# A two-layer diffusion block in split FP32: two more units of two FFNs as seven half-size products, the sums for them earlier, the dot products of the adaptive weights later

## The chip, the cores and the metric

One core of a Trainium2 chip runs the whole program as one launch. The metric is the device time of one execution in microseconds (us). Of the kernel before three runs are shown: 1622.91, 1625.24 and 1625.51, median 1625.24.

The engines that matter here: TensorE (PE) multiplies matrices, VectorE (DVE) and ScalarE (ACT) work on elements, SyncE (SP) issues the transfers. Each executes its own instructions in the order in which they were written into its queue, and waits on semaphores for the others.

## The reference

Two layers work on 256 image tokens ("LAT" in the kernel) and 256 context tokens ("CTX"), width 1024. Each layer has an FFN, a mixer (attention, then an mLSTM) and another FFN, each followed by a normalised residual. Shifts, scales and gates come from nine "adaptive" vectors a layer, `silu(c) @ ada_w`, for two conditions.

```python
def half_ffn(h, shift, scale, gate, w_in, w_out, g, b):
    xm = modulate(h, shift, scale)
    a, u = jnp.split(xm @ w_in, 2, axis=-1)
    y = (jax.nn.silu(a) * u) @ w_out
    return post_norm(h, 0.5 * gate * y, g, b)
...
        mod_lat = jnp.split((jax.nn.silu(c) @ ada_w[i] + ada_b[i])[:, None, :], N_MOD, axis=-1)
        mod_ctx = jnp.split((jax.nn.silu(c_ctx) @ ada_w[i] + ada_b[i])[None, None, :], N_MOD, axis=-1)
```

`w_in` is 1024 x 5632 and `w_out` 2816 x 1024. All inputs are FP32.

## The kernel before

**Precision.** A product in FP32 is made of three matmuls (`mm3`, line 241): every operand is split into a high part, a cast on ACT (line 225), and a low part, a subtraction on DVE (line 230, both in `split`). High by high, high by low, low by high are added up in PSUM. The weights are split on the fly: a raw tile of 128x1024 comes in by DMA (three raw slots, tag `raw`), the parts go into one of seven buffers (tag `w`).

**An FFN.** The 2816 hidden columns are 22 units of 128 (`j`). A plain unit (`unit_in`) multiplies its columns of both halves of `w_in` with all 512 tokens: 48 matmuls with 512 columns of tokens, then `ffn_g` applies silu (ACT, line 588), the product (DVE, line 589) and splits the result. After units 0 to 10 come eight out rows (`unit_out(0, d, ...)`, 33 matmuls of 512), then units 11 to 21, and eight more out rows that end in four narrow ones for each half of the tokens, into which the next normalisation is woven. In the second and third FFN (`li` 1 and 2) the units 0 to 3 are woven into the work ahead, and units 4 to 10 run plainly.

**Half-size units.** In the second and third FFN units 11 to 21 are made by `fast_in`: the weight of a unit is a 2x2 block of (half of the input width, half of the output), the tokens are a 2x2 block of (half of the width, LAT or CTX), and seven products of half size replace eight. That is 84 matmuls of 256 columns. It takes three sums of token blocks (`made`, from `fast_sums`, lines 611 to 623) that are made once, and four sums of the weight's blocks for every unit (s1, s2, s4, s3, line 641), whose parts are then split. PE accumulates in x, y, v and z; ACT copies halves out (lines 666 to 671) and DVE adds (lines 675 to 680). `fast_sums` also replaces the CTX tokens of the lower half of the width by LAT minus CTX, so no plain unit can follow. The sums are made beside out rows 4 and 5 of the first half, in memory that the pieces of `ada_w` held till then. One of the three sums is copied by ACT into a `w` buffer for unit 11 (line 635).

**Dots.** A piece of `ada_w` (128 rows of its transpose, 512 KB) is multiplied with silu(c) and added up on DVE (`ada_dot`, line 350), once for each condition. The table `DOTS` says how many pieces are loaded beside each unit and out row; `flush` issues the dots of the pieces of the step before.

**Order.** A list scheduler writes each engine's order from the program's order, with its own idea of durations; on the chip these orders are fixed.

Of the kernel before, what the change touches and what calls it, by code (L numbers as in the profile page):

```python
# [18 lines left out]
P = 128  # L19
# [7 lines left out]
NF = 22  # L27
# [61 lines left out]
SUMSAT = 4  # L89
# [4 lines left out]
    1: {**{("in", j): 2 for j in range(11)}, **{("out", 0, d): 2 if d < 2 else 1 for d in range(4)}, **{("out", 1, d): 1 for d in range(4)}},  # L94
    2: {**{("in", j): 2 for j in range(4)}, **{("in", j): 3 if j < 9 else 2 for j in range(4, 11)}, **{("out", 0, d): 2 if d < 3 else 0 for d in range(4)},
        **{("out", 1, d): 2 if d < 3 else 1 for d in range(4)}},
# [76 lines left out]
class Body:  # L173
    def __init__(self, ctx, tc, a, out):
        self.tc, self.nc, self.a, self.out = tc, tc.nc, a, out
        self.n = 0
        self.sp = ctx.enter_context(tc.tile_pool(name="sp", bufs=1))
        self.pp = ctx.enter_context(tc.tile_pool(name="pp", bufs=1, space=PSUM))
        self.later, self.running = [], []
        self.fence = {}  # L180
        self.fine = False

        self.nraw, self.spare = 0, None

# [104 lines left out]
    def silu_c(self):  # L289

        pool = ExitStack()
        self.n += 1
        p = pool.enter_context(self.tc.tile_pool(name=f"cp{self.n}", bufs=1, side="right"))
        self.cp = p
        self.cb = self.t([P, 2, D], pool=p)
        return pool
# [5 lines left out]
    def silu_all(self):  # L302
        pool = self.silu_c()
        self.silu_load()
        self.silu()
        return pool
# [285 lines left out]
    def fast_operands(self, st):  # L592

        n = ND // 2 * TL
        x = self.t([P, 6 * n], F32R, pool=st)
        self.t([P, FLIP], pool=st)
        self.made = [[x[:, (2 * i + p) * n : (2 * i + p + 1) * n].rearrange("p (k f) -> p k f", f=TL) for p in range(2)] for i in range(3)]

    def fast_sums(self, i):
# [5 lines left out]
        def at(ks, g):  # L605
            return self.xh[:, ks, g[0] : g[1]], self.xl[:, ks, g[0] : g[1]]

        def whole(ks, g):
            o = self.tmp().rearrange("p (k f) -> p k f", k=2)
            h, l = at(ks, g)  # L610
            V.tensor_tensor(out=o, in0=h.bitcast(F32), in1=l.bitcast(F32), op=ALU.add)
# [3 lines left out]
        V.tensor_tensor(out=a, in0=a, in1=b, op=ALU.subtract)  # L615
        self.split(a, *at(lo, CTX))
# [3 lines left out]
        V.scalar_tensor_tensor(a, a, -1.0, c, ALU.mult, ALU.subtract)  # L620
        self.split(a, *made(0))
        d = whole(up, LAT)
        V.scalar_tensor_tensor(d, a, -1.0, d, ALU.mult, ALU.subtract)
        self.split(d, *made(2))

    def fast_in(self, j, w_in, st):
# [4 lines left out]
        if j == NFH:  # L631
# [17 lines left out]
        self.split(sums[:, : 2 * half], *ws[2])  # L649
        self.split(sums[:, 2 * half :], *ws[3])  # L650
# [33 lines left out]
    def ffn(self, layer, s, gate, groups, side, start=None, cpool=None):  # L684
# [4 lines left out]
        with self.tc.tile_pool(name=f"ffn{li}", bufs=1) as gp:  # L689
# [34 lines left out]
            for hf in range(2):  # L724
# [26 lines left out]
                fast = cpool is not None and hf == 1  # L751
                for j in js:
                    if fast:
                        self.fast_in(j, w_in, st)
                        continue
                    unit_in(j, stream(j), allg)
                    assert not self.running
                    if j >= LEAD + FAFTER:
                        self.fine = False
                    call("in", j)  # L760
                    self.residual(2, self.pin)
                if not hf:
# [3 lines left out]
                if fast:  # L766
                    more.close()
                    cpool = self.silu_all()
                for d in range(body):
                    if cpool and not hf and d == SUMSAT:  # L770
                        self.flush()
                        cpool.close()
                        self.n += 1
                        more = ExitStack()
                        st = more.enter_context(self.tc.tile_pool(name=f"st{self.n}", bufs=1, side="right"))
                        self.fast_operands(st)
                    unit_out(hf, d, w, allg)
                    if cpool and not hf and d >= SUMSAT and d - SUMSAT < 2:
                        self.fast_sums(d - SUMSAT)
                    call("out", hf, d)  # L780
                if body < ND:
                    w = Keep(self, w.chunks, SH, w)
                    self.fine = True
                    for g in groups:
                        for d in range(body, ND):
                            unit_out(hf, d, w, g, TAILSTEP)
                    self.steps('B')
        return cpool
# [846 lines left out]
def emit(ctx, tc, a, out):  # L1635
# [4 lines left out]
    cpool = b.silu_c()  # L1640
    both2 = (0, 1)
    queue = [(0, p, both2) for p in range(16, 72)]
    later = [(1, p, both2) for p in range(40)] + [(1, p, (0,)) for p in range(40, 72)]
    made = {}
# [8 lines left out]
    def side(key, coef, keep=(True, True), nxt=True, alone=False, dots={}):  # L1653
        def pop():
            for _ in range(3 if len(queue) > 40 else 2):
                if queue:
                    b.ada(*queue.pop(0))

        def some(n):
            b.flush()  # L1660
            for _ in range(min(n, len(later))):
                layer, dt, vecs = later.pop(0)
# [6 lines left out]
        for j in range(NF):  # L1669
            s["in", j] = (lambda j=j: some(dots.get(("in", j), 0))) if dots else pop  # L1670
        for d in range(ND):
            s["out", 0, d] = (lambda d=d: some(dots.get(("out", 0, d), 0))) if dots else pop
            s["out", 1, d] = lambda d=d: some(dots.get(("out", 1, d), 0))
# [109 lines left out]
```

## Time and profile before

| what | number |
|---|---|
| median of three runs | 1625.24 us |
| the profiled execution, its span | 1624.66 us, 1622.9 us |
| PE, DVE, ACT busy | 1608.2, 1349.3, 749.0 us |
| second FFN, units 4 to 10 | 602.08 to 678.24 us |
| second FFN, units 11 to 21 | 738.11 to 843.11 us |
| third FFN, units 11 to 21 | 1090.08 to 1195.08 us |

Times in the trace count from the span's start. A busy PE is a PE with a matmul in flight; where it waits for an operand, its row or its stretch shows less than the whole. An operation on DVE or ACT is listed with its full length, and the next can start before that has passed, so the step from start to start is read from the timeline. Names of tiles are shown without numbers in the trace (`t<-t,t`), so operations are told by line and shape.

### The profile page before, as it was taken

To read this page: it belongs to the slowest core of one execution; us is meant where nothing else is said; L and a number is where in the kernel's file an instruction comes from. 1 tells how busy PE (TensorE), PEld (TensorE's weight loads), DVE (VectorE), ACT (ScalarE), POOL (GpSimd) and SP (SyncE) were. 2 spreads that over 40 slices of the span, in tenths; PEclk is the share of its full clock that TensorE was granted. 3 is DMA by queue.
4 is the path that set the end of the run, shared out by engine and by line. 5 is a ranking of instruction groups with operands and counts; after the bars stand their busy time and mean duration, and the time that the engine had idled before them with its cause. 6 is when DMAs were issued, how large, how long until landed. Compare 5 with 4: busy or idle time off the path is not lost. (4 is left out here: it accounts for less than half of the span.)

```text
span 1622.9 us, 26548 instructions
## 1 busy us (share of the span) xinstructions
PE 1608.2 (99%) x10280; PEld 1450.3 (89%) x10280; DVE 1349.3 (83%) x2687; ACT 749.0 (46%) x1276; POOL 62.4 (4%) x77
## 2 busy tenths in 40 slices
PE   9999999999999999999999999999999999999998
PEld 7888888889988998889999998889999989999986
DVE  7899978648879879999976979689967968897597
ACT  6522132314676443316652443336642657566542
POOL 0000000001011200000000100000001000020000
PEclk9999999999999999999999999999999999999999
DMA  9677765422203347633354258723372343437562
GB/s 358 220 250 238 237 207 184 141 66 85 66 2 99 136 144 228 212 104 118 117 175 151 79 180 289 245 64 106 109 238 83 98 130 92 151 98 259 170 181 91
DMA packets 72222, 251.56 MB, mean 155 GB/s; under 512 B 7960, under 2 KB 10776, under 8 KB 72096
## 3 DMA queue, kind: packets, MB, share of 16 engines
q1 hardware_dynamic: 71520, 249.09, 48.0%
q8 instruction: 80, 1.31, 0.3%
q10 hardware_dynamic: 576, 0.79, 0.1%
q14 instruction: 46, 0.38, 0.1%
HBM read 248.79 MB, written 1.05 MB: 154 GB/s over the span
## 5 line engine op out<-in xcount | busy, mean ns | idle before, releaser
L241 PE MATMUL t<-t,t 128*128 128x256 f32 (+2 forms) x8340 | 1307.7, 318 | 3.2 <-ACT t L225 1.1
L241 PEld LDWEIGHTS t<-t,t 128*128 128x128 f32 x8340 | 1175.8, 188 | 120.7 <-ACT t L225 2.0
L225 ACT CAST t<-t 128x1024 fp32r<-128x1024 f32 (+3 forms) x509 | 421.6, 850 | 479.3 <-PE t L241 225.0
L230 DVE TENSOR_TENSOR t<-t,t 128x256 fp32r<-128x256 f32 (+2 forms) x728 | 505.4, 729 | 110.7 <-ACT t L225 106.9
L350 DVE SCALAR_TENSOR_TENSOR t<-t,t 128x1024 bf16<-128x1024 f32 x224 | 260.7, 1220 | 0.0
L588 ACT ACTIVATE t<-t 128x512 f32<-128x512 f32 (+1 forms) x71 | 34.4, 489 | 98.8 <-PE t L241 97.8
L941 PE MATMUL t<-t,t 128*128 128x256 f32 (+1 forms) x256 | 79.3, 310 | 0.2 <-ACT t L541 0.2
L718 DVE SCALAR_TENSOR_TENSOR t<-t,t,t 128x256 f32<-128x256 f32 x96 | 42.7, 478 | 43.9 <-PE t L241 43.7
L943 PE MATMUL t<-t,t 128*128 128x256 f32 (+1 forms) x256 | 78.5, 307 | 0.1
L942 PE MATMUL t<-t,t 128*128 128x256 f32 (+1 forms) x256 | 78.3, 306 | 0.1
L589 DVE TENSOR_TENSOR t<-t,t 128x512 f32<-128x512 f32 (+1 forms) x71 | 39.0, 553 | 40.6 <-PE t L241 27.7
L484 POOL TENSOR_TENSOR t<-t,t 128x256 f32<-128x256 f32 x30 | 23.2, 774 | 1105.1 <-ACT t L474 1103.8
L869 PE MATMUL t<-t,t 128*128 128x512 f32 (+1 forms) x300 | 61.0, 364 | 0.4 <-DVE t L863 0.4
L869 PEld LDWEIGHTS t<-t,t 128*128 128x128 f32 x300 | 51.3, 189 | 10.0 <-DVE t L863 1.1
L474 ACT ACTIVATE t<-t 128x256 f32<-128x256 f32 x72 | 26.1, 412 | 65.8 <-DVE t L467 65.8
L1470 PE MATMUL t<-t,t 128*128 128x512 f32 (+2 forms) x276 | 55.7, 357 | 0.0
L1470 PEld LDWEIGHTS t<-t,t 128*128 128x128 f32 (+1 forms) x276 | 44.9, 183 | 11.0 <-issue 1.1
L942 PEld LDWEIGHTS t<-t,t 128*128 128x128 f32 x256 | 48.1, 188 | 3.3 <-DVE t L230 0.8
L941 PEld LDWEIGHTS t<-t,t 128*128 128x128 f32 x256 | 48.2, 188 | 3.2 <-ACT t L541 0.4
L943 PEld LDWEIGHTS t<-t,t 128*128 128x128 f32 x256 | 48.1, 188 | 2.8 <-DVE t L542 0.3
L541 ACT ACTIVATE t<-t,t 128x256 fp32r<-128x256 f32 x72 | 32.8, 502 | 31.1 <-DVE t L540 31.1
L641 DVE TENSOR_TENSOR t<-t,t 128x512 f32<-128x512 f32 x66 | 45.3, 687 | 0.4
(211 smaller groups left out, 1107.8 us busy)
## 6 DMA issues: line engine op xcount, KB each, us to landing
t<-in_ffn_in SPq DMA_DIRECT2D x168, 512.0 KB, 4.1
t<-in_ada_w SPq DMA_DIRECT2D x138, 512.0 KB, 4.4
t<-in_ffn_out SPq DMA_DIRECT2D x66, 512.0 KB, 4.4
t<-in_ffn_last SPq DMA_DIRECT2D x22, 512.0 KB, 3.5
t<-in_att_in SPq DMA_DIRECT2D x12, 512.0 KB, 3.5
t<-in_att_out SPq DMA_DIRECT2D x8, 512.0 KB, 3.6
t<-in_ml_qk SPq DMA_DIRECT2D x8, 512.0 KB, 3.7
t<-in_ml_v SPq DMA_DIRECT2D x8, 512.0 KB, 3.6
```

The source lines that it names most:

```text
L225: self.behind(self.nc.scalar.copy(h, x))
L230: self.behind(self.nc.vector.tensor_tensor(out=ls, in0=xs, in1=hs.bitcast(F32), op=ALU.subtract))
L241: mm = lambda *k, **kw: self.nc.tensor.matmul(*k, skip_group_check=not group, **kw)
L350: ins = nc.vector.scalar_tensor_tensor(self.tmp().bitcast(BF16), r, 1.0, self.cb[:, v, :], ALU.mult, ALU.mult, accum_out=to)
L589: V.tensor_tensor(out=sl, in0=sl, in1=pu[:, :n], op=ALU.mult)
L641: add = lambda o, x, y: V.tensor_tensor(out=o, in0=x, in1=y, op=ALU.add)
L718: V.scalar_tensor_tensor(z, y[:, gg[0] - t0 : gg[1] - t0], gate()[:, v, d : d + 1], z, ALU.mult, ALU.add)
L869: pin(nc.tensor.matmul(o, gs[g], ws[k][w][:, i : i + n], start=k == k0 and g == w == 0, stop=k == k1 - 1 and g == 1,))
L941: mm(o, self.xh[:, k, c], wh, start=k == 0, stop=False)
L942: mm(o, self.xh[:, k, c], wl, start=False, stop=False)
L943: mm(o, self.xl[:, k, c], wh, start=False, stop=k == ND - 1)
L1470: mm = lambda *k, **kw: pin(nc.tensor.matmul(*k, **kw))
```

## The change

In the second and third FFN units 9 and 10 are made by `fast_in` as well. For that the token sums (`fast_sums`) move from out rows 4 and 5 to beside units 6 and 7, and the splits of the difference LAT minus CTX, which overwrite tokens, come as `fast_first` beside unit 8, ahead of unit 9. The table `FAST` gives the first half-size unit and the unit beside which the sums start. The pieces of `ada_w` lose their memory from unit 6 on, so `DOTS` puts dots beside units 0 to 4 and then beside the out rows, where the pieces take halves of `w` buffers. Silu(c) keeps its memory and is no longer loaded again. The sums of a unit's weights are four tiles of 512 and no longer one of 2048, and two splits of 1024 become four of 512. The copy of a token sum for PE is made for units 9 and 11. In the first FFN a piece's dots now come one step behind its load.

```diff
-SUMSAT = 4
+FAST = {0: (99, 99), 1: (9, 6), 2: (9, 6)}
...
     def ada_load(self, layer, dt):
...
-        r = self.t([P, 1024], tag="ada", bufs=PIECES, pool=self.cp)
+        if self.cp:
+            r = self.t([P, 1024], tag="ada", bufs=PIECES, pool=self.cp)
+        else:
+            self.halves = self.halves or self.pair(F32)
+            r = self.halves.pop()
...
         a, b = whole(lo, LAT), whole(lo, CTX)
-        V.tensor_tensor(out=a, in0=a, in1=b, op=ALU.subtract)
-        self.split(a, *at(lo, CTX))
+        for k in range(2):
+            o = self.first[2 * i + k] = self.t([P, TL], tag="s1", bufs=S1B)
+            V.tensor_tensor(out=o, in0=a[:, k, :], in1=b[:, k, :], op=ALU.subtract)
...
+    def fast_first(self):
+        for k in range(ND // 2):
+            self.split(self.first[k], *self.x(k, CTX))
...
-        sums = self.t([P, 4 * half], tag="sums", bufs=1, pool=st)
...
-        s1, s2, s4, s3 = (part(sums, i) for i in range(4))
+        s1, s2, s4, s3 = (self.tmp() for _ in range(4))
...
-        self.split(sums[:, : 2 * half], *ws[2])
-        self.split(sums[:, 2 * half :], *ws[3])
+        for i, x in enumerate((s1, s2, s4, s3)):
+            self.split(x, *(part(y, i % 2) for y in ws[2 + i // 2]))
...
-                    if fast:
-                        self.fast_in(j, w_in, st)
-                        continue
-                    unit_in(j, stream(j), allg)
+                    if j >= fast:
+                        self.fast_in(j, w_in, j in (fast, NFH))
+                    else:
+                        unit_in(j, stream(j), allg)
...
-                    call("in", j)
+                    if j <= sums:
+                        call("in", j)
                     self.residual(2, self.pin)
+                    if j == sums:
+                        self.fast_operands()
+                    if sums <= j < sums + 2:
+                        self.fast_sums(j - sums)
+                    if j == fast - 1:
+                        self.fast_first()
...
                             unit_out(hf, d, w, g, TAILSTEP)
+                            self.flush()
```

DVE's order at the end of the second FFN's unit 8, before. Row 819 is unit 8's product (`t_6458`), rows 817, 818 and 820 are low parts of weights, rows 822 to 825 dots:

```order
817 L230 TENSOR_TENSOR t_6653<-t_6651,t_6653 128x1024
818 L230 TENSOR_TENSOR t_6682<-t_6680,t_6682 128x1024
819 L589 TENSOR_TENSOR t_6458<-t_6458,t_6397 128x512
820 L230 TENSOR_TENSOR t_6729<-t_6727,t_6729 128x1024
821 L230 TENSOR_TENSOR t_6457<-t_6458,t_6456 128x512
822 L350 SCALAR_TENSOR_TENSOR t_6463,t_6126<-t_6388,t_5394 128x1024
823 L350 SCALAR_TENSOR_TENSOR t_6465,t_6126<-t_6388,t_5394 128x1024
824 L350 SCALAR_TENSOR_TENSOR t_6467,t_6126<-t_6390,t_5394 128x1024
825 L350 SCALAR_TENSOR_TENSOR t_6469,t_6126<-t_6390,t_5394 128x1024
```

and after (lines are nine to sixteen higher). Row 831 is the last operation of the moved sums, row 833 unit 8's product; `t_6507` and `t_6509` are unit 9's raw tiles, `t_6515` the low part of a11, `t_6516` of a12 and a22, `t_6517` of s1 and s2, and lines 657 are the sums s1, s2, s4, s3:

```order
831 L231 TENSOR_TENSOR t_68<-t_6409,t_67 128x256
832 L657 TENSOR_TENSOR t_6511<-t_6507,t_6509 128x512
833 L598 TENSOR_TENSOR t_6487<-t_6487,t_6426 128x512
834 L231 TENSOR_TENSOR t_6515<-t_6507,t_6515 128x512
835 L231 TENSOR_TENSOR t_6516<-t_6509,t_6516 128x1024
836 L231 TENSOR_TENSOR t_6486<-t_6487,t_6485 128x512
837 L572 SCALAR_TENSOR_TENSOR t_66<-t_66,t_5324,t_5665 128x256 x2
838 L657 TENSOR_TENSOR t_6512<-t_6511,t_6507 128x512
839 L231 TENSOR_TENSOR t_6517<-t_6511,t_6517 128x512
840 L657 TENSOR_TENSOR t_6513<-t_6512,t_6509 128x512
841 L657 TENSOR_TENSOR t_6514<-t_6507 128x512
842 L231 TENSOR_TENSOR t_6517<-t_6512,t_6517 128x512
```

The dots are gone from here, the moved sums stand ahead of unit 8's product, and unit 9's low parts stand behind it.

Further on in DVE's order after: `t_6640` and `t_6642` are unit 10's raw tiles, `t_6649` the low part of its a12 and a22, `t_6650` of its s1; lines 691 to 696 are the end of unit 9:

```order
845 L231 TENSOR_TENSOR t_6648<-t_6640,t_6648 128x512
846 L657 TENSOR_TENSOR t_6644<-t_6640,t_6642 128x512
847 L691 TENSOR_TENSOR t_6538<-t_6538,t_6536 128x512
848 L231 TENSOR_TENSOR t_6649<-t_6642,t_6649 128x1024
849 L695 SCALAR_TENSOR_TENSOR t_6539<-t_6535,t_6539 128x512
850 L657 TENSOR_TENSOR t_6645<-t_6644,t_6640 128x512
851 L696 TENSOR_TENSOR t_6538<-t_6538,t_6539 128x512
852 L657 TENSOR_TENSOR t_6646<-t_6645,t_6642 128x512
853 L657 TENSOR_TENSOR t_6647<-t_6640 128x512
854 L231 TENSOR_TENSOR t_6633<-t_6538,t_6632 128x512
855 L572 SCALAR_TENSOR_TENSOR t_66<-t_66,t_5324,t_5665 128x256 x2
856 L231 TENSOR_TENSOR t_6650<-t_6644,t_6650 128x512
```

Unit 10's s1 has its sum in row 846 and its low part in row 856, ten rows behind. Before, a plain unit's two low parts stood here (rows like 818).

PE's order at the start of unit 9, before (`t_6480` and `t_6481` are its two sums in PSUM, `t_6484` its first weight; the third matmul takes the low part):

```order
3409 L241 MATMUL t_6480<-t_67,t_6484 128x512
3410 L241 MATMUL t_6480<-t_68,t_6484 128x512
3411 L241 MATMUL t_6480<-t_67,t_6484 128x512
3412 L241 MATMUL t_6481<-t_67,t_6484 128x512
3413 L241 MATMUL t_6481<-t_68,t_6484 128x512
```

after, from the last matmul of unit 8 on (`t_6535` is x, `t_6536` y and v, `t_6537` z, `t_6504` the copied token sum):

```order
3408 L242 MATMUL t_6426<-t_67,t_6458 128x512
3409 L242 MATMUL t_6535<-t_67,t_6515 128x256
3410 L242 MATMUL t_6535<-t_68,t_6515 128x256
3411 L242 MATMUL t_6536<-t_67,t_6516 128x256
3412 L242 MATMUL t_6536<-t_68,t_6516 128x256
3413 L242 MATMUL t_6537<-t_6504,t_6516 128x256 x2
3414 L242 MATMUL t_6535<-t_67,t_6515 128x256 x2
```

and in the middle of unit 10 (`t_6669` takes s1, `t_6670` z, `t_6668` s2, `t_6777` is the first out row):

```order
3469 L242 MATMUL t_6669<-t_67,t_6650 128x256
3470 L242 MATMUL t_6669<-t_68,t_6650 128x256
3471 L242 MATMUL t_6670<-t_6308,t_6649 128x256 x2
3472 L242 MATMUL t_6668<-t_6308,t_6650 128x256 x2
3473 L242 MATMUL t_6670<-t_6308,t_6649 128x256 x10
3474 L242 MATMUL t_6777<-t_5509,t_6780 128x512
3475 L242 MATMUL t_6777<-t_5510,t_6780 128x512
3476 L242 MATMUL t_6669<-t_67,t_6650 128x256 x2
```

Six matmuls of unit 9 that take high parts of the weights stand ahead of the first that takes a low part; in unit 10 two of s1's stand ahead of z's, s2's first two and two matmuls of the first out row, and s1's third, with the low part, behind them.

## Rows read from the trace of the kernel before

**Rows 1.** The profile's page: busy time of each engine, clock by slices.

```profile
PE 1608.2 (99%) x10280; PEld 1450.3 (89%) x10280; DVE 1349.3 (83%) x2687; ACT 749.0 (46%) x1276; POOL 62.4 (4%) x77
...
PEclk9999999999999999999999999999999999999999
```

**Rows 2.** Table of stretches: start:end length, busy (count) by engine, PEclk, DMA share, GB/s.

```profile
602.08:656.48 54.40, 54.40 (x242) 45.05 (x241) 52.45 (x85) 19.37 (x29) 0.00 (x0) 1.00 0.76 227
656.48:678.24 21.76, 21.76 (x97) 18.02 (x96) 18.61 (x33) 8.27 (x13) 0.00 (x0) 1.00 0.68 219
...
738.11:843.11 105.00, 105.00 (x926) 105.00 (x924) 97.20 (x129) 67.15 (x109) 0.00 (x0) 1.00 0.39 122
1090.08:1195.08 105.00, 105.00 (x925) 105.00 (x924) 95.44 (x128) 67.16 (x110) 0.00 (x0) 1.00 0.41 122
```

**Rows 3.** DVE's groups by form, whole span: count, then busy us, mean ns, idle before.

```profile
L230 DVE TENSOR_TENSOR t<-t,t 128x1024 fp32r<-128x1024 f32 x236 | 286.8, 1222 | 65.7 <-ACT t L225 62.7 <-PE t L241 1.7
L350 DVE SCALAR_TENSOR_TENSOR t<-t,t 128x1024 bf16<-128x1024 f32 x224 | 260.7, 1220 | 0.0
L230 DVE TENSOR_TENSOR t<-t,t 128x256 fp32r<-128x256 f32 x346 | 132.8, 426 | 40.4 <-ACT t L225 40.2
L230 DVE TENSOR_TENSOR t<-t,t 128x512 fp32r<-128x512 f32 x133 | 90.8, 686 | 4.1 <-ACT t L225 3.5
...
L563 DVE SCALAR_TENSOR_TENSOR t<-t,t,t 128x256 f32<-128x256 f32 x64 | 28.0, 479 | 0.0
```

**Rows 4.** DVE's timeline in a half-size unit: start, length, instruction [idle before <-releaser].

```profile
1102.57 0.69 DVE L641 TENSOR_TENSOR t<-t,t 128x512 f32<-128x512 f32 x1
1103.17 0.69 DVE L641 TENSOR_TENSOR t<-t 128x512 f32<-128x512 f32 x1
1103.77 0.69 DVE L230 TENSOR_TENSOR t<-t,t 128x512 fp32r<-128x512 f32 x1
```

**Rows 5.** DVE's timeline around the second FFN's units 6 to 9.

```profile
633.67 0.87 DVE L563 SCALAR_TENSOR_TENSOR t<-t,t,t 128x256 f32<-128x256 f32 x2
...
635.61 0.69 DVE L589 TENSOR_TENSOR t<-t,t 128x512 f32<-128x512 f32 x1
636.22 1.82 DVE L230 TENSOR_TENSOR t<-t,t 128x1024 fp32r<-128x1024 f32 x2
...
654.09 2.35 DVE L230 TENSOR_TENSOR t<-t,t 128x1024 fp32r<-128x1024 f32 x2
656.78 0.69 DVE L589 TENSOR_TENSOR t<-t,t 128x512 f32<-128x512 f32 x1 [0.34 <-PE t L241]
```

**Rows 6.** DVE's timeline beside the second FFN's fifth out row.

```profile
713.76 1.89 DVE L611 TENSOR_TENSOR t<-t,t 128x512 f32<-128x512 f32 x3
715.57 0.69 DVE L615 TENSOR_TENSOR t<-t,t 128x512 f32<-128x512 f32 x1
...
716.96 0.68 DVE L230 TENSOR_TENSOR t<-t,t 128x512 fp32r<-128x512 f32 x1
```

**Rows 7.** ACT's timeline at the same place.

```profile
716.29 0.62 ACT L225 CAST t<-t 128x512 fp32r<-128x512 f32 x1 [14.96 <-DVE t L615]
```

**Rows 8.** The page's DMA issues: line, KB each, us to landing.

```profile
t<-in_ffn_in SPq DMA_DIRECT2D x168, 512.0 KB, 4.1
...
t<-in_ffn_out SPq DMA_DIRECT2D x66, 512.0 KB, 4.4
```

**Rows 9.** ACT's groups by form, whole span.

```profile
L225 ACT CAST t<-t 128x1024 fp32r<-128x1024 f32 x309 | 323.4, 1051 | 388.0 <-PE t L241 220.3 <-issue 92.5 <-DMA t<-in_ffn_in 43.1
```

**Rows 10.** DVE's timeline in the second FFN's last out rows.

```profile
869.52 1.43 DVE L230 TENSOR_TENSOR t<-t,t 128x256 fp32r<-128x256 f32 x4
...
874.05 0.75 DVE L424 TENSOR_TENSOR t<-t,t 128x256 f32<-128x256 f32 x2
...
885.45 0.42 DVE L424 TENSOR_TENSOR t<-t,t 128x256 f32<-128x256 f32 x1
```

More of the change, by code (lines that the diff above doesn't have):

```diff
@@ L765, in ffn @@
                 body = ND - TAIL if hf else ND
-                if fast:
-                    more.close()
-                    cpool = self.silu_all()
+                self.halves = []
+                if hf and fast < NF:
+                    self.shut()
+                    self.cp = self.open()
                 for d in range(body):
[L770 to L776, printed above, removed]
                     unit_out(hf, d, w, allg)
-                    if cpool and not hf and d >= SUMSAT and d - SUMSAT < 2:
-                        self.fast_sums(d - SUMSAT)
                     call("out", hf, d)
+                self.halves = []
                 if body < ND:
@@ L1639, in emit @@
     b.setup_rest()
-    cpool = b.silu_c()
+    b.silu_c()
     both2 = (0, 1)
@@ L1643, in emit @@
     later = [(1, p, both2) for p in range(40)] + [(1, p, (0,)) for p in range(40, 72)]
+    later, queue = queue[56 - 0 :] + later, queue[: 56 - 0]
     made = {}
@@ L1653, in side @@
     def side(key, coef, keep=(True, True), nxt=True, alone=False, dots={}):
[L1654 to L1657, printed above, removed]
         def some(n):
             b.flush()
-            for _ in range(min(n, len(later))):
-                layer, dt, vecs = later.pop(0)
+            todo = queue or later
+            for _ in range(min(n, len(todo))):
+                layer, dt, vecs = todo.pop(0)
                 b.waiting.append((b.ada_load(layer, dt), layer, dt, vecs))
@@ L1669, in side @@
         for j in range(NF):
-            s["in", j] = (lambda j=j: some(dots.get(("in", j), 0))) if dots else pop
+            s["in", j] = lambda j=j: some(dots.get(("in", j), 0))
         for d in range(ND):
-            s["out", 0, d] = (lambda d=d: some(dots.get(("out", 0, d), 0))) if dots else pop
-            s["out", 1, d] = lambda d=d: some(dots.get(("out", 1, d), 0))
+            for hf in range(2):
+                s["out", hf, d] = lambda hf=hf, d=d: some(dots.get(("out", hf, d), 0))
         return s
     both = (LAT, CTX)
-    b.ffn(0, 0, once("g0", lambda: b.half_gate(0, 2)), both, side("n0", lambda: b.ln_mod(0, 0, (0, 3))), start)
-    assert not queue
-    cpool.close()
+    b.ffn(0, 0, once("g0", lambda: b.half_gate(0, 2)), both, side("n0", lambda: b.ln_mod(0, 0, (0, 3)), dots=DOTS[0]), start)
+    assert not queue, len(queue)
+    b.flush()
+    b.shut()
+    b.shut()
     b.attention(lambda: b.shift_(0, 5), side("n1", lambda: b.ln_mod(0, 1, (0, 6))))
-    cpool = b.silu_all()
-    cpool = b.ffn(0, 1, once("g1", lambda: b.half_gate(0, 8)), both, side("n2", lambda: b.ln_mod(0, 2, (1, 0)), dots=DOTS[1]), cpool=cpool)
-    cpool = b.ffn(1, 0, once("g2", lambda: b.half_gate(1, 2)), both, side("n3", lambda: b.ln_mod(1, 0, (1, 3)), (True, False), dots=DOTS[2]), cpool=cpool)
+    b.silu_all()
+    b.ffn(0, 1, once("g1", lambda: b.half_gate(0, 8)), both, side("n2", lambda: b.ln_mod(0, 2, (1, 0)), dots=DOTS[1]))
+    b.ffn(1, 0, once("g2", lambda: b.half_gate(1, 2)), both, side("n3", lambda: b.ln_mod(1, 0, (1, 3)), (True, False), dots=DOTS[2]))
     assert not later, len(later)
     b.flush()
-    cpool.close()
+    b.shut()
+    b.shut()
     b.mlstm(lambda: b.shift_(1, 5, slice(0, 1)), side("n4", lambda: b.ln_mod(1, 1, (1, 6), 1), alone=True))
```

56 lines of the change are left out of this document (31 added, 25 removed).

## The prediction

> **What bounds the kernel now.** First the page: TensorE (PE) is busy 99% of the span and its clock stands at full speed in nearly every slice, so a second is saved where PE gets less to do and lost where it has to wait [rows 1]. Then the table of stretches. It shows the second FFN's plain units 4 to 8 and 9 and 10, the eleven half-size units of the second FFN, and those of the third. PE is busy through all of them at a granted clock of 1.00. VectorE (DVE) is busy 52.45 of 54.40 us beside the plain units and 97.20 and 95.44 of 105.00 us beside the half-size ones [rows 2]. So PE is the bound, with DVE close behind, and DVE feeds PE: each weight's low part is a DVE subtraction that PE waits for.
>
> From the same table, 96 matmuls of 512 columns take 21.76 us, 0.2267 us each, and a plain unit (48 of them) 10.88 us. A half-size unit has 84 matmuls of 256 columns; eleven have 924 and fill 104.7 of the 105.00 us (the rest is the edge's 512-wide ones): 0.1133 us each, 9.52 us a unit [rows 2].
>
> **The gain.** Units 9 and 10 of two FFNs go from 10.88 to 9.52 us: 4 x 1.36 = 5.44 us, if PE waits no more than it did.
> [...]
>
> **DVE in a half-size unit.** Before: nine 512-wide operations and three 1024-wide ones. After: thirteen and one (two wide subtractions became four half ones). One 512-wide lasts 0.686 us, a 1024-wide 1.222, a dot 1.220 [rows 3], but in a run of 512-wide ones each starts 0.60 us after the one before [rows 4], and two 1024-wide ones take 2.35 us, so the second starts some 1.14 us behind the first [rows 5]. So 9 x 0.60 + 3 x 1.14 = 8.8 before and 13 x 0.60 + 1.14 = 8.9 after, both under 9.52: the steady run stays PE's, cost 0.
> [...]
>
> **Unit 9: late weights.** This is the main cost. Before, DVE is through with unit 6's product at 636.22 and then does weights and dots [rows 5]. DVE's order after is the same up to there; then come the sums of the tokens with what else stands between: 21 operations of 512, 6 plain and 8 three-operand ones of 256. Steps: 0.60 (the token sums beside the rows show it too: three in 1.89 [rows 6]); 0.40 for a three-operand one (a pair in 0.87, of which the last 0.479 [rows 3, 5]); 0.34 for a plain one of 256 (four in 1.43, the last 0.426 [rows 3, 10]). That is 12.6 + 2.0 + 3.2 = 17.8 us, to 654.1. The low parts inside need a cast by ScalarE (ACT) first: from the sum's start at 715.57 over the cast at 716.29 to the low part at 716.96 is 1.39 us [rows 6, 7], and two to three other operations stand between each time, so no more than 0.3 is lost.
>
> Behind these stand, in order, s1's sum for unit 9 and the product of unit 8, which can't start before unit 8 ends: 656.78, as in the row that waits for PE [rows 5]. Only behind it come unit 9's own low parts. a11: 657.38 to 658.07. PE is done with unit 8 at 656.5 and can do six half matmuls that need no low part (0.7), so it waits from 657.2 to 658.1: 0.9. Then a12 and a22 together (to 659.1), unit 8's low part (659.7), two residual operations (660.5), s2's sum, s1's low part (661.8), s4's and s3's sums, s2's low part (to 663.6). PE, late by 0.9, wants s2's at 663.2: 0.5 more. Together 1.4, say 1.5 (0.8 where a step comes earlier, 2.4 where a cast on ACT is in the way of another).
>
> **Unit 10: the same and a transfer.** Its second raw tile goes into the slot that unit 9's s4 sum reads last, done at 662.4. The transfer takes 4.1 us [rows 8], so it is there at 666.5, and s1's sum waits for it. Behind that in DVE's queue come the sum of unit 9's halves, the 1024-wide low part, the rest of unit 9's end (residual, product, its low part) and the sums s2, s4, s3: ten steps, 6.8 us, so s1's low part runs 673.25 to 673.9. PE, begun at 667.5, has 40 half matmuls and two of the first out row in front (4.5 + 0.45): 672.5. It waits 1.6. What can add: ACT casts the first out row's chunks (1.05 each, [rows 9]) between the copies out of PSUM that PE's last two products need, and these chunks are transfers of 4.4 us [rows 8]; they just fit by my walk. I take 2.0 (0.8 to 3.8). So the second FFN loses 3.5. The third has the same order with five 128x16 operations more in the chain: 4.0. Together 7.5 (3 to 12).
>
> **Token sums no longer beside out rows; dots there instead.** An out row (33 matmuls, 7.48 us) now has four dots of 1.15, two gated additions of 0.40 and 11/8 low parts of 1.14: 7.0 us, hidden, with 0.5 to spare. In the last rows a piece's dots are flushed after each 256-wide row: before, two dots stand ahead of that row's addition and the last sum for the mean is made at 885.45 [rows 10]. After, from 874.7, when the pair at 874.05 is through: four dots (4.6), an addition and a sum (0.74), four dots (4.6), two additions and sums (1.5) make 886.2 against 885.9, and PE's order has the mean's matmul later by ten half matmuls. +0.5 (0 to 1). The first FFN's dots change only when their tile is loaded: 0. Two reloads of silu(c) vanish off the path: 0.
>
> **Sum.** -5.44 + 7.5 + 0.5 = +2.6 us. The profiled execution took 1624.66, so 1627.3; the median of the runs shown, 1625.24, is 0.58 above that execution: 1627.8.
>
> **Rivals.**
> A. The weights are in time, or nearly: DVE's backlog shrinks where a wait that I counted overlaps. For it: PE has not one idle microsecond in units 4 to 10 with DVE 96% busy [rows 2], and the scheduler chose an order in which only a11's low part is late. Against it: unit 8's product can't be earlier and stands ahead. It gives -5.44 + (0 to 1.8) + 0.5: 1620.3 to 1622.1.
> B. Slower in earnest: the chain of raw slots. There are three; unit 10's second weight, then the first out row's chunks each wait for a slot that a late sum reads last. If a copy out of PSUM waits in ACT's queue behind a cast whose chunk isn't there, PE stands for the transfer's rest and the cast (up to 4.4 + 1.05 less the 2 us of work at hand, some 3.5) in each FFN: +2.6 + 7 = +9.6, 1634.8. It decides from the point where the chunk lands over 2 us later than 672. For it: seven weight buffers hold nine pairs' worth around unit 9. Against it: the chunks are asked for at 662.
> C. DVE's steps are full durations where forms alternate. 26 units of 0.6 us: +16, about 1641. The runs of [rows 4] speak against it.
>
> **Numbers.** Forecast 0.57 (stalls 3.5 to 9.5 in sum: 1623.8 to 1629.8), A 0.23, B 0.16, C 0.04. Under 0.2%, 3.25 us, a measurement can't tell from no change: 1622.0 to 1628.5 is the same. Faster: most of A, 0.18. Slower: B, C and the third of the forecast above 1628.5, 0.39. Same 0.43. The range 1621.0 to 1634.0 leaves out the best of A and the upper half of B, with C: under 2 in 10.
>
> **What would show it.** In the profile after: PE idle at the start of units 9 and 10 of both FFNs, released by DVE's low part (line 231), 1 to 2.5 us each, and no idle in the eleven units behind; DVE's unit 8 product directly before unit 9's first low part; 84 matmuls of 0.1133 us in units 9 and 10. Wrong would be: no PE idle there (A), ACT's cast or the in_ffn_out transfer as releaser of PE's waits (B), or half-size units of over 9.6 us throughout (C). Then the time falls out of the forecast's own range.

## The result, and the profile after

The changed kernel takes 1628.08 us (median of eight runs, 1625.34 to 1630.55), the kernel before 1625.03 beside it (eight runs, 1622.91 to 1626.32): a ratio of 1.0020, interval 1.0011 to 1.0030. That is 3 us slower and just inside of what was called the same; 1627.8 was forecast. Its runs spread over 5.2 us, those of before over 3.4.

Where the time went is read by cutting both traces at the same matmuls (starts of units and rows). The changed kernel was profiled twice (the second time among the experiments), the kernel before three times. Lengths in us:

| stretch | before, three profiles | changed | changed again |
|---|---|---|---|
| 2nd FFN, units 9, 10 and first out row | 29.24 each | 29.96 | 30.05 |
| units 11 to 21 | 105.00 each | 106.15 | 105.00 |
| last rows and the norm in them | 33.84 to 34.13 | 34.43 | 34.15 |
| 3rd FFN, lead (units 0 to 3) | 46.87, 46.88, 47.15 | 47.16 | 49.10 |
| units 9, 10 and first out row | 29.24 each | 29.26 | 29.36 |
| units 11 to 21 | 105.00 each | 105.38 | 105.00 |
| last rows | 33.82 to 34.12 | 34.31 | 34.49 |

All other stretches of the two FFNs agree within 0.01. Ahead of the second FFN's unit 4 and behind the third FFN one kernel's own profiles differ by up to 2.5, so nothing is read there.

The page after: PE has 144 more matmuls and 2.3 us less of busy time [rows 1], and the transfers are as long as before [rows 8].

```profile
PE 1605.9 (99%) x10424; PEld 1455.0 (90%) x10424; DVE 1376.1 (85%) x2783; ACT 768.0 (47%) x1356; POOL 62.2 (4%) x77
...
t<-in_ffn_in SPq DMA_DIRECT2D x168, 512.0 KB, 4.1
```

The same table of stretches after, for the second FFN's units 4 to 8, its units 9, 10 and first row, its run of half-size units, the third FFN's lead and its units 9, 10 and first row. PE is idle where it never was in [rows 2]: 1.54 and 1.23 us beside units 9 and 10, at a granted clock of 1.00.

```profile
601.65:656.08 54.43, 54.43 (x243) 45.05 (x241) 52.12 (x94) 21.10 (x36) 0.00 (x0) 1.00 0.36 111
656.08:686.04 29.96, 28.42 (x203) 26.29 (x201) 25.91 (x39) 20.06 (x36) 0.00 (x0) 1.00 0.53 197
738.40:844.54 106.14, 105.85 (x925) 105.65 (x924) 100.63 (x152) 69.45 (x131) 0.00 (x0) 1.00 0.36 125
908.92:956.08 47.16, 46.44 (x399) 45.94 (x397) 37.27 (x106) 22.61 (x49) 2.31 (x3) 1.00 0.36 109
1010.50:1039.76 29.26, 28.03 (x202) 25.89 (x201) 24.83 (x38) 18.05 (x34) 0.00 (x0) 1.00 0.57 224
```

PE's timeline at units 9 and 10 of the second FFN (in brackets the idle time before the row and what ended it):

```profile
657.18 13.62 PE L242 MATMUL t<-t,t 128*128 128x256 f32 x110 [0.71 <-ACT t L226]
671.25 1.65 PE L242 MATMUL t<-t,t 128*128 128x256 f32 x12 [0.45 <-ACT t L682]
673.24 27.02 PE L242 MATMUL t<-t,t 128*128 128x512 f32 x139 [0.34 <-ACT t L226]
```

In terms of single matmuls against their steps: 0.98 us before the first that takes a12, 0.32 before s2's first, 0.73 before s2's first in unit 10, 0.62 before the first out row's. These four waits, each with what the next matmul loses, make 2.65 of the 3.44 us that the stretch takes beyond 26.52 (29.24 less the gain of 2.72). Most of the rest is no wait: nearly all half-wide matmuls there start 0.118 us apart and not 0.113, at a granted clock of 1.00. DVE's timeline there answers to [rows 5]: s1's sum, unit 8's product (waiting for PE), unit 9's low parts behind it, the sums, then unit 10's s1, which waits for its transfer, the sum of unit 9, s2's sum at 668.99, and from 672.79 on s1's low part:

```profile
654.53 0.68 DVE L657 TENSOR_TENSOR t<-t,t 128x512 f32<-128x512 f32 x1
656.35 0.69 DVE L598 TENSOR_TENSOR t<-t,t 128x512 f32<-128x512 f32 x1 [1.13 <-PE t L242]
656.95 2.42 DVE L231 TENSOR_TENSOR t<-t,t 128x512 fp32r<-128x512 f32 x3
...
661.29 0.69 DVE L657 TENSOR_TENSOR t<-t,t 128x512 f32<-128x512 f32 x1
...
666.04 0.69 DVE L657 TENSOR_TENSOR t<-t,t 128x512 f32<-128x512 f32 x1 [1.02 <-DMA t<-in_ffn_in]
666.65 0.69 DVE L691 TENSOR_TENSOR t<-t,t 128x512 f32<-128x512 f32 x1
...
668.99 0.68 DVE L657 TENSOR_TENSOR t<-t,t 128x512 f32<-128x512 f32 x1
...
672.79 5.90 DVE L231 TENSOR_TENSOR t<-t,t 128x512 fp32r<-128x512 f32 x7
```

And ACT's: the two copies of the token sum, a11's cast, unit 8's silu, then a12 and a22's cast as the first of three; further on two casts, the first of which waits for s2's sum, and the copy of unit 10's x:

```profile
653.09 2.00 ACT L652 CAST t<-t 128x1024 fp32r<-128x1024 f32 x2
655.00 0.61 ACT L226 CAST t<-t 128x512 fp32r<-128x512 f32 x1
655.60 0.60 ACT L597 ACTIVATE t<-t 128x512 f32<-128x512 f32 x1
656.09 2.12 ACT L226 CAST t<-t 128x1024 fp32r<-128x1024 f32 x3
...
669.70 1.22 ACT L226 CAST t<-t 128x512 fp32r<-128x512 f32 x2 [1.56 <-DVE t L657]
670.83 0.36 ACT L682 COPY t<-t 128x256 f32<-128x256 f32 x1
```

The walk's times are hit within 0.5 us (656.35, 666.04 and 672.79 against 656.78, 666.5 and 673.25, with PE 0.43 ahead at unit 4 already). But ACT ends three of PE's four waits, not DVE: a12's high part is cast behind the copies of the last token sum, and x's copy stands behind two casts. DVE is not out of it: unit 10's x is complete at 668.9, and the first of the casts ahead of its copy waits 1.56 us for s2's sum, which stands in DVE's queue behind the late s1.

### The profile page after: what moved, and what is told of

It is laid out like the page before. It is cut to its first block, busy times and chain, and to the rows that moved or that the text cites. A ratio compares the mean times of both kernels' runs of the same rounds, so it can differ in the third digit from the quotient of the medians.

```text
span 1625.2 us, 26955 instructions
## 1 busy us (share of the span) xinstructions
PE 1605.9 (99%) x10424; PEld 1455.0 (90%) x10424; DVE 1376.1 (85%) x2783; ACT 768.0 (47%) x1356; POOL 62.2 (4%) x77
## 5 line engine op out<-in xcount | busy, mean ns | idle before, releaser
L226 ACT CAST t<-t 128x1024 fp32r<-128x1024 f32 (+3 forms) x573 | 436.9, 785 | 454.9 <-PE t L242 133.5
L231 DVE TENSOR_TENSOR t<-t,t 128x256 fp32r<-128x256 f32 (+3 forms) x792 | 517.0, 689 | 100.1 <-ACT t L226 97.1
L597 ACT ACTIVATE t<-t 128x256 f32<-128x256 f32 (+1 forms) x67 | 32.0, 483 | 98.1 <-PE t L242 97.0
L598 DVE TENSOR_TENSOR t<-t,t 128x256 f32<-128x256 f32 (+1 forms) x67 | 36.3, 545 | 36.9 <-PE t L242 31.1
L657 DVE TENSOR_TENSOR t<-t,t 128x512 f32<-128x512 f32 x78 | 53.6, 687 | 2.2 <-DMA t<-in_ffn_in 1.5
```

Of the source, the lines that this page charges most:

```text
L226: self.behind(self.nc.scalar.copy(h, x))
L231: self.behind(self.nc.vector.tensor_tensor(out=ls, in0=xs, in1=hs.bitcast(F32), op=ALU.subtract))
L598: V.tensor_tensor(out=sl, in0=sl, in1=pu[:, :n], op=ALU.mult)
L657: add = lambda o, x, y: V.tensor_tensor(out=o, in0=x, in1=y, op=ALU.add)
```

## The experiments

All runs are beside runs of the kernel before on the same chip; ratios are to those.

**e1: all but the two units.**
```diff
-FAST = {0: (99, 99), 1: (9, 6), 2: (9, 6)}
+FAST = {0: (99, 99), 1: (11, 6), 2: (11, 6)}
```


> All of the change but its units: half-size products from unit 11 on, token sums still beside units 6 and 7, dots still beside the out rows. In the changed kernel's trace the stretch from unit 9 to the end of the first out row costs, against the kernel before, +0.7 us in the second FFN and 0.0 in the third (gain 2.72 each, waits 3.4 and 2.7); what lies elsewhere costs +1.6 (1.1 and 0.4 in the two runs of units 11 to 21, 0.3 at the second FFN's tail, 0.3 in the third's lead, -0.4 ahead of unit 4). Theory 'late weights at 9 and 10, and a thin prefetch in the steady run': the units give nothing on balance, so without them the time stays 1 to 2 us above the kernel before (about 1626.5), with some 1 us of PE's waits left in the runs of units 11 to 21. Theory of the prediction alone (all of the loss at units 9 and 10, 0.5 at the tail): 0.5 us above it, 1625.5, and runs of 105.0 us. Theory 'the moved dots cost it': 3 us above it, 1628.

Measured: 1629.08 against 1625.77, ratio 1.0021 (1.0012 to 1.0031). The stretches of units 9 and 10 are 29.24 again, runs 105.00, tails 34.67 and 34.68, lead 47.29. So the units are worth nothing that shows, near what the tally in the expectation had, but the rest costs 3.4 us (1.9 to 5.0) and not 0.5: the nearest of the three was the moved dots. The profile shows 1.5 of it in the two tails and the lead; where the remainder lies, in the parts that are not read, stays open.

**e2: s3 first among a unit's weight sums.**
```diff
         add(s1, a21, a22)
         add(s2, s1, a11)
         add(s4, s2, a12)
-        add(s3, a11, a21)
```
(the removed line now stands ahead of s1's)


> The four weight sums of a half-size unit in another order: s3, s1, s2, s4 in place of s1, s2, s4, s3. Now a unit's first raw tile is read last by s2 and not by s3, it comes free before the second, and the tiles go round in the three slots: each load waits for the tile three loads back (before this edit a unit's second tile waits for the unit before's second one, two loads back). Theory 'thin prefetch': in the second FFN's run of units 11 to 21 the last load is issued several us earlier than at 822.5, ACT waits for weights there under 1 us in all (5.7 us in the changed kernel), the run takes 105.0 us and not 106.1, the third FFN's 105.0 and not 105.4; unit 10's second tile is asked for 0.6 to 1.2 us earlier, so its wait shrinks by as much in each FFN. Time 1.5 to 4 us below the changed kernel: 1624 to 1626.5. Rival 'DVE's and ACT's own order sets the late units': runs of 106 as before, time within 0.7 us of 1628.

Measured: 1639.47, ratio 1.0082 (1.0066 to 1.0098); runs of 111.05 and 108.97. The theory's forecast failed. ACT in the run, unit 20's load on its way: the cast waits for the transfer, silu and x's copy of the unit before stand behind it:

```profile
819.38 1.05 ACT L226 CAST t<-t 128x1024 fp32r<-128x1024 f32 x1 [1.04 <-DMA t<-in_ffn_in]
820.34 0.62 ACT L692 ACTIVATE t<-t 128x512 f32<-128x512 f32 x1
820.87 0.35 ACT L682 COPY t<-t 128x256 f32<-128x256 f32 x1
822.42 0.62 ACT L226 CAST t<-t 128x512 fp32r<-128x512 f32 x1 [1.20 <-DVE t L696]
```

DVE at the same time: the product behind that silu (821.71), its low part, which waits for ACT, and only then s3 and the other sums:

```profile
814.38 1.41 DVE L657 TENSOR_TENSOR t<-t,t 128x512 f32<-128x512 f32 x2
...
821.71 0.68 DVE L696 TENSOR_TENSOR t<-t,t 128x512 f32<-128x512 f32 x1
823.07 0.69 DVE L231 TENSOR_TENSOR t<-t,t 128x512 fp32r<-128x512 f32 x1 [0.69 <-ACT t L226]
823.68 0.68 DVE L657 TENSOR_TENSOR t<-t 128x512 f32<-128x512 f32 x1
824.28 1.41 DVE L657 TENSOR_TENSOR t<-t,t 128x512 f32<-128x512 f32 x2
```

The last sum (s2) frees the raw slot, and the load for it is issued at 825.76; the one before was issued at 815.85. So load, cast, silu, product, low part, sums and the next load make a ring of 9.91 us, longer than a unit's 9.52, and PE waits for x's copy:

```profile
832.40 4.37 PE L242 MATMUL t<-t,t 128*128 128x256 f32 x36 [0.73 <-ACT t L682]
...
843.92 6.42 PE L242 MATMUL t<-t,t 128*128 128x256 f32 x51 [1.22 <-ACT t L682]
```

The order of four additions thus sets the pace of 11 units: with this edit a unit's first load follows the one before after 9.90 or 9.91 us at most places of both runs. In the changed kernel the ring is just short enough: where transfers take 3.4 to 3.6 us, that step is 9.32 or 9.33 us at most places, 0.2 less than a unit. So a long transfer can show (106.15 in one profile, 105.00 in the other). In the first profile the load at 822.46 takes 5.04 us, and x's copy waits behind the cast of that weight:

```profile
827.52 1.05 ACT L226 CAST t<-t 128x1024 fp32r<-128x1024 f32 x1 [1.39 <-DMA t<-in_ffn_in]
828.48 0.36 ACT L682 COPY t<-t 128x256 f32<-128x256 f32 x1
```

```profile
828.89 21.28 PE L242 MATMUL t<-t,t 128*128 128x256 f32 x156 [0.29 <-ACT t L682]
```

Of the 1.15 us that this run loses, 0.56 stand at that wait; the rest is again steps of 0.118 us in place of 0.113, from there to the run's end. The kernel before lost nothing in any run of its three profiles and e5's, loads of 4.46 us (at 805.12) and 4.59 us (at 1113.42) in the first of these included.

**e3: token sums one unit earlier.** `FAST` (9, 5) in both FFNs.


> Token sums beside units 5 and 6 and no longer 6 and 7. DVE's order then has unit 9's first low parts (a11, and a12 with a22) ahead of unit 8's product, because the sums are done a unit earlier. Theory 'DVE's queue at unit 9 is full of sums': PE's wait at the start of unit 9 (0.7 us seen, 1.7 in all from unit 9's start to unit 10's) goes to under 0.5 in both FFNs; unit 10's wait for its second tile and the steady run stay as they are. Time about 2.5 us below the changed kernel: 1625.5. Rival 'unit 8's product and the copies of the token sum on ACT set it, whatever DVE does': unit 9 still takes over 11 us, time within 0.7 of 1628. A third outcome, that the earlier sums push the low parts of units 6 to 8 late: units 7 and 8 over 10.95 us, time above 1628.

Measured: 1626.88, ratio 1.0009 (0.9999 to 1.0019). The stretches fall to 27.71 and 27.61, within 1.2 of 29.24 - 2.72 = 26.52, but unit 8 is 1.0 longer in both FFNs. PE's timeline shows its second tile's low part late behind the sums (653.53):

```profile
653.53 18.32 PE L242 MATMUL t<-t,t 128*128 128x512 f32 x134 [0.70 <-DVE t L231]
672.15 18.22 PE L242 MATMUL t<-t,t 128*128 128x256 f32 x106 [0.30 <-DVE t L231]
```

So the sums in DVE's queue do make units 9 and 10 late, though ACT ended the wait; moved earlier they delay what stands there.

**e4: e2 and e3 together.** `FAST` (9, 5) with s3 first.


> Both edits: token sums beside units 5 and 6, and weight sums in the order s3, s1, s2, s4. If the two causes are separate, the gains add: unit 9 near 9.6 us, unit 10 and the first out row near 17.3, runs of units 11 to 21 at 105.0; time 1621.5 to 1623.5, below both kernels. If they are one cause seen twice, it is as good as the better of the two alone, about 1625. The steps' own price, with no wait at all, would be 5.4 below the kernel before: 1619.6, plus 0.3 at the tail.

Measured: 1635.61, ratio 1.0057 (1.0044 to 1.0070): stretches 26.91 and 27.09, runs 108.58 and 109.10. The two effects come together, but e2's is a loss. They don't simply add: s3 first makes the stretches 0.24 and 0.13 longer alone, and 0.80 and 0.52 shorter once the sums are earlier.

**e5: the late dots alone, in the kernel before.**
```diff
-        **{("out", 1, d): 2 if d < 3 else 1 for d in range(4)}},
+        **{("out", 1, d): 4 if d < 2 else 2 for d in range(4)}},
...
                             unit_out(hf, d, w, g, TAILSTEP)
+                            self.flush()
```
(and two a row in the second FFN, with as many fewer beside the plain units)


> The kernel before with one part of the change alone: more dots beside the last out rows (second FFN two pieces a row in place of one, third four, four, two, two in place of two, two, two, one, and as many fewer beside the plain units), and the pending dots flushed after each narrow row. Units 9 and 10 are plain, the token sums stand where they stood. Seen so far: with all of the change but its two units the time is 3.3 us above the kernel before, and in its trace the tails of the two FFNs take 34.67 and 34.68 us in place of 34.13 and 34.12, the third FFN's lead 47.29 in place of 46.87. Theory 'the late dots hold up the normalisations': tails and lead as there, the time 1.2 to 3.5 us above the kernel before. Rival 'it is the smaller sum tiles and the pieces in the weight buffers, or only the spread of transfers': tails at 34.1, time within 0.8 us of the kernel before.

Measured: 1626.58 against 1625.36, ratio 1.0005 (0.9996 to 1.0014); tails 34.62 and 33.82, lead 47.84. Between the theories.

**e6: half-size from unit 10 on.** `FAST` (10, 6).


> Half-size products from unit 10 on (unit 9 plain again), token sums still beside units 6 and 7. DVE's order then has unit 10's first low parts ahead of unit 9's product. Theory 'late weights because the sums stand directly ahead': the stretch from unit 9 to the end of the first out row takes 29.24 - 1.36 = 27.9 us plus under 0.7 of waits in both FFNs, where the changed kernel takes 29.96 and 29.26 with twice the gain. Time 0.7 to 2 us below the changed kernel. Rival 'any first half-size unit waits 1.5 us, since PE's matmuls of the next unit's low parts come at its start': 29.0 to 29.5 and the changed kernel's time.

Measured: stretches 28.50 and 28.51, so 1.36 gained and 0.62 lost in each, as expected; but the time is 1628.36, ratio 1.0019 (1.0010 to 1.0028), as the changed kernel's, and not 0.7 to 2 us below. Its tails, 34.97 and 35.10, are longer than the changed kernel's.

**e7: token sums beside units 4 and 5.** `FAST` (9, 4).


> Token sums beside units 4 and 5, two units ahead of where the change has them; units 9 and 10 as in the change. With the sums beside 5 and 6 the stretch of units 9, 10 and the first out row went from 29.96 and 29.26 us to 27.71 and 27.61, but unit 8 became 1.0 us longer, as its own low part came late behind the sums. Now DVE has three units between the sums and unit 9. Theory 'it is DVE's backlog': unit 8 back at 10.9 us, units 9 and 10 with the first row at 27.7 or less, units 4 to 6 perhaps longer by under 1 us; 1.0 to 3 us below the changed kernel. Rival 'the backlog only moves': what unit 8 gains units 5 and 6 lose, time as with the sums beside 5 and 6 (1626.9).

Measured: 1638.54, ratio 1.0078 (1.0064 to 1.0092). Units 9 and 10 with the row are 27.82 and 27.74, but units 4 to 8 take 59.73 and 60.96 in place of 54.43: the dots of the units before still fill DVE there, which is busy without a gap from 620 to 650. PE waits once for 3.61 us in each FFN, and the granted clock behind the second FFN's wait is 0.72 in the mean from 650 to 656, and 0.994 over the whole profile, where the changed kernel's first has 0.999:

```profile
650.43 39.94 PE L242 MATMUL t<-t,t 128*128 128x512 f32 x247 [3.61 <-DVE t L231]
```

Both expectations missed the size.

**e8: the changed kernel again.**


> The changed kernel once more, for a second profile. A stretch that differs between two profiles of the same kernel by more than 0.3 us is the execution's, not the kernel's. Theory 'transfers that PE's waits hang on last 3.4 to 5.1 us, and the changed kernel has more such places': the run of units 11 to 21 of the second FFN, the third FFN's lead and the part behind the third FFN differ from the first profile (106.15, 47.16 and 363.42 us) by 0.3 to 3 us, the stretches of units 9, 10 and the first row by under 0.3. Rival 'the losses are fixed by the order': all stretches agree within 0.2 us, and the median stays near 1628.

Measured: 1628.41, ratio 1.0020 (1.0011 to 1.0029). Units 9 and 10 agree within 0.1; the run and the lead don't. The lead in ACT's timeline, first profile, second profile: a weight's cast waits for its transfer, and four squares for the norm's sums (line 483) wait behind the cast.

```profile
917.32 1.05 ACT L226 CAST t<-t 128x1024 fp32r<-128x1024 f32 x1 [0.48 <-DMA t<-in_ffn_in]
918.27 1.34 ACT L483 ACTIVATE t<-t 128x256 f32<-128x256 f32 x4
```

```profile
917.65 1.05 ACT L226 CAST t<-t 128x1024 fp32r<-128x1024 f32 x1 [1.40 <-DMA t<-in_ffn_in]
918.60 1.34 ACT L483 ACTIVATE t<-t 128x256 f32<-128x256 f32 x4
```

The transfer took 3.52 us in one and 4.44 in the other, for 512 KB each. PE's timeline of the second shows its wait, and the table in steps of 2 us what followed:

```profile
921.45 1.05 PE L456 MATMUL t<-t,t 128*128 128x1 f32 x8 [0.86 <-DVE t L493]
922.37 5.27 PE L242 MATMUL t<-t,t 128*128 128x256 f32 x30
```

```profile
918.00:920.00 2.00, 2.00 (x20) 2.00 (x19) 0.41 (x2) 2.00 (x6) 0.77 (x2) 1.00 0.08 33
920.00:922.00 2.00, 1.14 (x11) 0.94 (x9) 2.00 (x6) 0.44 (x2) 0.78 (x1) 1.00 0.00 0
922.00:924.00 2.00, 2.00 (x14) 2.00 (x14) 2.00 (x8) 0.68 (x3) 0.00 (x0) 0.69 0.26 94
924.00:926.00 2.00, 2.00 (x11) 2.00 (x11) 1.69 (x11) 0.18 (x1) 0.00 (x0) 0.50 0.67 227
926.00:928.00 2.00, 2.00 (x17) 1.95 (x16) 0.51 (x2) 0.00 (x0) 0.00 (x0) 0.95 0.52 199
928.00:930.00 2.00, 2.00 (x19) 2.00 (x18) 1.62 (x4) 1.17 (x3) 0.00 (x0) 1.00 0.01 4
```

PE is idle 0.86 us from 920.6, and from 922 to 926 the granted clock reads 0.69 and then 0.50. Over all profiles with the late dots the lead is 47.2 to 47.8 at a clock of 1.00 (five) or 49.1 to 50.1 at 0.97 (four); the transfer takes 3.4 to 3.7 us in those and 4.4 to 5.1 in these.

**f1: no dots beside the last eight out rows.**
```diff
-                s["out", hf, d] = lambda hf=hf, d=d: some(dots.get(("out", hf, d), 0))
+                s["out", hf, d] = lambda hf=hf, d=d: (left if hf and dots in (DOTS[1], DOTS[2]) else some)(dots.get(("out", hf, d), 0))
```
(`left` writes a constant and loads nothing)


> The changed kernel without the dots beside the last eight out rows of the second and third FFN: their pieces are neither loaded nor multiplied, GpSimd writes a constant in their place (so 22 of 72 pieces of the second layer's vectors are not computed, and 11 MB less come in). With all of the change but its units the time was 3.3 us above the kernel before; more late dots alone, in the kernel before, made 0.8 to 1.2. Theory 'late dots and their transfers are the larger part of what the change costs outside of units 9 and 10': tails of 34.1 us and a lead near 46.9, and the time 2 to 3.5 us below the changed kernel, 1625 to 1626.5. Rival 'they are a third of it': 0.5 to 1.5 below, 1627 to 1628. Rival 'the lead's and the rest's spread comes from transfers whatever else is there': tails at 34.1, but the lead still 47.2 to 50 and the time within 1 us of 1628.3.

Measured: 1626.46 against 1624.68, ratio 1.0012 (1.0002 to 1.0022); tails 34.12 and 34.11, lead 46.84. That is 0.0008 of the time, 1.3 us, below the changed kernel: tails and lead came as the first theory had them, the time, by the ratios, as 'a third of it'. DVE's rows in the changed kernel's tail answer to [rows 10]: a narrow row's addition (line 734) comes behind four dots, and the last sum for the mean (line 433) at 888.07, where it was 885.45. Of these 2.6 us, 1.44 come from ahead of the tail (its first matmul is at 874.49, before at 873.05); the other 1.2 are the tail's own, made by the dots: in f1 that sum stands 12.4 us behind the tail's first matmul, as in the kernel before, and here 13.6:

```profile
880.97 0.48 DVE L734 SCALAR_TENSOR_TENSOR t<-t,t,t 128x256 f32<-128x256 f32 x1
...
886.61 0.87 DVE L734 SCALAR_TENSOR_TENSOR t<-t,t,t 128x256 f32<-128x256 f32 x2
...
888.07 0.42 DVE L433 TENSOR_TENSOR t<-t,t 128x256 f32<-128x256 f32 x1
```

In the lead of f1 the cast stands ahead of no wait: ACT goes from the first four squares through it to the next four without idling.

```profile
915.03 1.39 ACT L483 ACTIVATE t<-t 128x256 f32<-128x256 f32 x4 [5.77 <-DVE t L476]
...
917.50 1.33 ACT L483 ACTIVATE t<-t 128x256 f32<-128x256 f32 x4
```

**f2, f3: the kernel before, two profiles more.**


> The kernel before once more, for a second profile. In eight profiles of kernels with the new dots the third FFN's lead took 47.2 to 47.4 us where one transfer lasted 3.4 to 3.7 us, and 49.1 to 50.1 where it lasted 4.4 to 5.1; the one profile of the kernel before has 46.87. Theory 'the change sets that transfer 0.3 to 0.6 us later and so on PE's path, the kernel before has room for it': the lead again 46.9, whatever the transfer lasts. Rival 'the same wait hangs over the kernel before': 46.9 with a short transfer, 48.5 or more with a long one.

> A third profile of the kernel before, as in the second: the lead at 46.9 with any transfer, or 48.5 and more with a long one. If all three show a short transfer, it stays open whether the kernel before has the room.

Measured: 1625.56 and 1624.05; leads 46.88 and 47.15, no transfer long. Whether the kernel before would bear a long one stays open. Its transfer is issued 4.46, 4.48 and 4.76 us behind the lead's start in its three profiles, 4.63 to 5.09 in the nine with the late dots, and 4.47 and 4.77 in f1 and g1 without them. So the late dots alone do not set it.

**g1: half-size from unit 10 on, without the late dots.** `FAST` (10, 6) in f1.


> Half-size products from unit 10 on, and no dots beside the last eight out rows of the second and third FFN (22 of 72 pieces of the second layer's vectors are left out, as in the run before this edit). It closes the account: if the time outside of units 9 and 10 goes to the late dots, and what is left there to the waits, this is the kernel before less 1.5 us (two stretches of 28.5 in place of 29.24), with tails of 34.1 and leads of 46.9: 0.5 to 2 us below the kernel before. If something else in the change costs 2 us (the four sum tiles, the pieces in the weight buffers, the sums beside units 6 and 7), the time is 0.5 to 2 us above it, and that cost stays open.

Measured: 1624.26 against 1625.70, ratio 0.9990 (0.9981 to 0.9999): 1.6 us faster, as the two stretches say (2 x 0.74). So the account closes, within the intervals, with the waits at units 9 and 10 and the late dots. But the runs of units 11 to 21 are not free: g1's profile loses 0.95 us in the second FFN's (its first load takes 5.00 us) and f1's 0.53 (behind a load of 5.12). Of the eight profiles with the changed kernel's order of weight sums three lose something there. It looks like a price of the new sums and splits of the weights (in the kernel before the loads of a run settle 9.52 us apart, at PE's own pace), but no run takes these alone, and what share of the median it makes is not shown. How much the late dots cost is not settled: 1.3 us by f1, 4.7 by e6 and g1 (ratios 1.0019 and 0.9990), and 0.8 for the like in the kernel before (e5), with intervals of 1.4 us and more to either side.

## Why the prediction came out

The time was right, in part by luck: its terms were wrong in opposite ways. The waits at units 9 and 10 came where they were forecast, but ACT ended three of the four, which the prediction had called a sign of being wrong, with a time outside of its range; the time stayed inside.

- **The gain, 5.44.** Right: units 11 to 21 still take 105.00 us, and e6's stretches show 1.36 a unit less a wait of 0.62.
- **DVE in the steady run, cost 0.** Right in the second profile; in the first the two runs lost 1.5, at x's copy on ACT behind the cast of a late transfer (0.9) and in longer steps behind that (0.6). The term counted DVE's work and not the ring of a load, 9.33 of 9.52 us. That is rival B's mechanism at another place; the price of B in full (9.6) did not come. C, whose 0.6 us a unit is 13 x 0.686 + 1.222 = 10.1 less 9.52 [rows 2, 3], did not come either: no run of 26 units loses 16.
- **Unit 9, 1.5.** Measured 11.26 us to unit 10's start in the second FFN and 11.14 in the third, less 9.52: 1.74 and 1.62. The size was right. The step 'a11's low part: PE waits 0.9' named the wrong engine: a12's high part on ACT came last, behind the token sum's copies that I had not walked through; a11's low part ended at 657.6, half a microsecond behind it and hidden.
- **Unit 10, 2.0 and more in the third FFN.** Measured 18.70 and 18.12 us with the first row, less 17.00: 1.70 and 1.12. The transfer landed as forecast (666.04), but s1's low part made PE wait for nothing: x's copy and the first chunk's cast on ACT had stopped PE until then. The five small operations in the third FFN cost nothing, so 4.0 was 2.7 there; the second FFN's 3.5 was 3.4. The chain that the step had walked, transfer and DVE's sums, did reach PE, through ACT's casts ahead of x's copy. Sum lost in the two stretches 6.2 (6.4 in the second profile) for 7.5.
- **The late dots, 0.5.** Mis-sized. The tails themselves lost 0.5 in the first profile (0.30 and 0.19; 0.02 and 0.37 in the second), but the step stopped at the mean's matmul. In the third FFN's lead behind it PE's path hangs on a transfer, and where that is long (4.4 to 5.1 us) PE waits (0.86 us in e8) and the granted clock of the lead is 0.97 in the mean: leads 2.2 to 3.3 us longer than the kernel before's 46.87, in four of nine executions with late dots and none of five without. That the late dots make the transfer late or long is not shown. The runs put the late dots at 0.8 to 4.7 us, and all of the change but its units at 3.4 (e1). What spreads the runs is open too: e5, with late dots alone, spreads over 2.7 us in eleven runs, and f1, without them, over 5.7.

So 7.5 was 1.1 to 1.3 too much, 0.5 was too little, by an amount that the runs do not settle, and the steady run's 0 left out up to 1.5: the sum hid all three. In two places where PE lost time ACT's rows show work held behind a cast in its queue: unit 10's x is complete at 668.9, and its copy starts at 670.83, behind casts of which the first had waited 1.56 us; and in the lead the norm's second four squares, the first of whose operands is made by 917.0, start at 918.27, behind a cast that had waited 0.48 us, and in e8 at 918.60, behind one that had waited 1.40.

## What to carry to other kernels

Follow a moved step through the queue of every engine that it passes, to the end of the work that it delays, and not to the first wait: here ACT's queue (x's copy 1.9 us behind x) and the next FFN's lead were left out. Count a buffer's whole ring, from a load over its last reader to the next load, against the steady step (here 9.33 and, in e2, 9.91 us against 9.52), and not only each engine's work. Profile a kernel twice before a microsecond in one stretch is explained; the two stretches that differed by over 1 us between two profiles here hung on a transfer. Work that is hidden behind PE in a steady stretch may not be hidden beside a normalisation, where PE itself waits for the small engines: here the late dots made a tail's last sum 1.2 us later, and in e8's lead PE waited 0.86 us for DVE.

## What the hardware showed

A transfer of 512 KB, with a second one issued 1.35 us behind it, lasted 3.4 to 5.1 us in the lead of nine profiles of nearly the same program; what lengthens it is open. After PE waits in the lead of 0.86 us (e8) and 1.79 us (e3) the granted clock read 0.50, for some 3.4 us by its means in steps of 2 us (0.69, 0.50, 0.95 and 0.77, 0.50, 0.88), which cost e8 1.6 us beside the wait (30 matmuls from 922.37 on took 5.27 us, in the first profile 3.67); in e4 and e7 it was 0.97 in the lead's mean. Beside units 9 and 10, with waits of up to 0.8 us, it stayed at 1.00. Each of the four waits at units 9 and 10 of the second FFN cost about 0.11 us more at the second matmul behind it (0.226, 0.224 and 0.221 us for 0.118, and 0.335 for the 512-wide 0.227). And at a granted clock of 1.00 half-wide matmuls started 0.113 us apart in most of the steady runs, but 0.118 behind the wait at 828.89 up to the run's end; behind the one of the third FFN's run, at 1106.26, they were back at 0.113 after a few. What sets the two steps is open.
